# Layer 0's input projection of a streaming encoder as seven block products (Strassen's identity, one level)

## Chip, cores and metric

One Trainium2 chip, one core, one launch. The metric is the device time in microseconds of one execution. Engines: PE (TensorE) multiplies, DVE (VectorE), ACT (ScalarE) and POOL (GpSimd) work on elements, SP issues the transfers.

## What is computed

The reference is a two-layer encoder on 1088 tokens (1024 of a prompt, 64 of a running stream), D = 1024, everything in 32-bit floats. Layer 0 is a gated short convolution, layer 1 latent attention. The part that matters here is layer 0:

```
h = rms_norm(x, g)
b_gate, c_gate, xv, z = split(h @ w_in, 4)          # w_in: 1024 x 4096
u = c_gate * xv
conv = sum over k = 0..2 of u[t - 2 + k] * conv_w[k]
x1 = x + (silu(z) * b_gate * conv) @ w_out
```

The two rows of `u` before the first token are zeros for the prompt and a stored state for the stream.

## The kernel before

Tokens lie on the free axis, features on the 128 partitions (KD = 8 tiles of 128). A 32-bit factor is split into `hi` (cast to fp32r) and `lo` (the rest), and each product is three matmuls: hi by hi, hi by lo, lo by hi. `load_w` does this for weights: SP loads 512 KB into `wraw` (three buffers), ACT casts to `whi` (line 288), POOL subtracts into `wlo` (line 292).

Layer 0 takes the 1088 tokens in three chunks, `CHK`: 384, 384 and 320. For each of 8 feature tiles `ct` and each of 4 parts (order `PARTS = [1, 2, 3, 0]`: c_gate, xv, z, b_gate) `conv_mm` runs for each chunk 8 times 3 matmuls into one of 8 PSUM banks, taken in turn by `gps`; that is 2304 matmuls. `conv_evac` takes the bank to SBUF: lines 440 and 444 make `u`, 451 to 453 silu(z), 457 to 467 the convolution (462, 464) with its operands in SBUF, the gate (465) and the split into `YH`, `YL` (466, 467).

`XH`, `XL` hold x times the gain g; the factor 1 / rms per token, `rb`, multiplies the results afterwards. For the first `ct` the order is written out by hand (`keep_order`, `pe_order`): the chunks of x are loaded, split (391, 392), squared and summed (397 to 401), `rstd` finds the factor by Newton steps on three columns (320 to 330), and `spread` brings it back to the columns with products with the identity. Everywhere else in layer 0 a scheduler of the compiler orders the instructions within each engine.

Then `conv_out` (1024 x 1024, 8 tiles times 3 chunks), the residual, and layer 1 with its projections and attention (from line 576 on).

## Time and profile before

| | |
|---|---|
| time, median of 3 executions | 1116.86 us (1115.74 to 1117.88) |
| the profiled execution: span from first to last instruction | 1115.8 us |
| PE busy | 1075.0 us, 96% of the span |
| DVE, ACT, POOL busy | 56%, 45%, 37% |
| layer 0's input projection on PE | from 5.78 to 403.62 us |

For the profiled execution the profile has the span alone, no separate time; it lies within the three times above. PE's row counts from the start of a matmul to its modelled end, and matmuls overlap, so the distance between two starts is what a matmul costs in a stream. The granted clock stands beside the engines' times: 1.00 is 2.4 GHz, 0.50 is 1.2 GHz.

### The profile page before, as it was taken

To read this page: it belongs to the slowest core of one execution; us is meant where nothing else is said; L and a number is where in the kernel's file an instruction comes from. 1 tells how busy PE (TensorE), PEld (TensorE's weight loads), DVE (VectorE), ACT (ScalarE), POOL (GpSimd) and SP (SyncE) were. 2 spreads that over 40 slices of the span, in tenths; PEclk is the share of its full clock that TensorE was granted. 3 is DMA by queue.
4 is the path that set the end of the run, shared out by engine and by line. 5 is a ranking of instruction groups with operands and counts; after the bars stand their busy time and mean duration, and the time that the engine had idled before them with its cause. 6 is when DMAs were issued, how large, how long until landed. Compare 5 with 4: busy or idle time off the path is not lost.

```text
span 1115.8 us, 17727 instructions
## 1 busy us (share of the span) xinstructions
PE 1075.0 (96%) x6659; PEld 1033.5 (93%) x6659; DVE 626.8 (56%) x1277; ACT 502.7 (45%) x1077; POOL 407.5 (37%) x375
## 2 busy tenths in 40 slices
PE   8989999999999999999898999999999999999994
PEld 7989999999999999999798999899999999989983
DVE  6752222222322235554898442688888888896456
ACT  6512121221112133344442334777887778785452
POOL 3123232323324232122433232354555445463243
PEclk9989999999999999999998999999999999999997
DMA  6211111111112123322323113444323422434324
GB/s 228 67 38 39 57 38 43 53 38 50 46 38 77 40 78 139 137 94 90 105 101 124 48 35 86 119 91 103 68 59 91 95 61 51 104 123 151 99 83 153
DMA packets 45461, 93.18 MB, mean 84 GB/s; under 512 B 6672, under 2 KB 23824, under 8 KB 45376
## 3 DMA queue, kind: packets, MB, share of 16 engines
q1 hardware_dynamic: 45168, 91.73, 27.4%
q8 instruction: 52, 0.85, 0.3%
q14 instruction: 33, 0.27, 0.1%
q10 hardware_dynamic: 144, 0.26, 0.1%
q0 software_dynamic: 64, 0.07, 0.0%
...
## 4 chain that ended last, share of the span: by engine, by line
PE 75%; DVE 8%; issue 5%; ACT 4%; DMA 4%; POOL 2%; SPq 1%; POOLq 0%; DVEq 0%; ACTq 0%
PE PS L298 55%; PE PS L1088 16%; PE PS L1127 4%; DMA QB<-stg 2%; POOL wlo L1366 1%; DVE rb L401 1%; ACT PH L1140 1%; DVE PL L1144 1%; SPq L1214 1%; DVE OL L612 1%; DMA wraw<-in_w 1%; ACT stg L1204 1%; DVE qt L813 0%; DVE SZ L364 0%; DVE qt L818 0%
## 5 line engine op out<-in xcount | busy, mean ns | idle before, releaser
L298 PE MATMUL PS<-XH,whi 128*128 128x384 f32 (+1 forms) x984 | 324.2, 329 | 4.7 <-DVE SZ L632 3.9
L298 PE MATMUL PS<-XL,whi 128*128 128x384 f32 (+1 forms) x984 | 322.8, 328 | 0.8 <-DVE XL L392 0.8
L298 PE MATMUL PS<-XH,wlo 128*128 128x384 f32 (+1 forms) x984 | 321.3, 328 | 0.0
L292 POOL TENSOR_TENSOR wlo<-wraw,whi 128x1024 fp32r<-128x1024 f32 x56 | 135.9, 2427 | 301.0 <-ACT whi L288 297.9
L298 PEld LDWEIGHTS PS<-XH,whi 128*128 128x128 f32 x984 | 185.9, 189 | 6.1 <-issue 4.1
L298 PEld LDWEIGHTS PS<-XL,whi 128*128 128x128 f32 x984 | 185.9, 189 | 2.2 <-DVE XL L392 1.8
L298 PEld LDWEIGHTS PS<-XH,wlo 128*128 128x128 f32 x984 | 185.7, 189 | 0.2
L1088 PE MATMUL PS<-KB,QB 96*128 96x512 f32 (+11 forms) x576 | 125.1, 354 | 0.9 <-DVE SZ L632 0.6
L288 ACT CAST whi<-wraw 128x1024 fp32r<-128x1024 f32 (+1 forms) x57 | 59.3, 1040 | 140.4 <-PE PS L298 127.9
L1088 PEld LDWEIGHTS PS<-KB,QB 96*128 96x128 f32 (+1 forms) x576 | 94.4, 190 | 9.3 <-DVE PL L1144 1.1
L1105 DVE TENSOR_REDUCE st<-PS 128x1 f32<-128x1024 f32 (+7 forms) x128 | 94.6, 747 | 10.7 <-PE PS L1088 10.0
L1144 DVE TENSOR_TENSOR PL<-PS,PH 128x512 fp32r<-128x512 f32 (+3 forms) x192 | 98.8, 547 | 3.2 <-ACT PH L1140 1.8
L1122 POOL TENSOR_SCALAR Pt<-Pt,st 128x640 f32<-128x640 f32 (+3 forms) x64 | 61.4, 961 | 85.9 <-DVE st L1118 85.3
L1140 ACT CAST PH<-PS 128x512 fp32r<-128x512 f32 (+3 forms) x192 | 85.3, 496 | 14.6 <-PE PS L1127 13.2
L1088 PE MATMUL PS<-PH,VB 128*128 128x256 f32 x320 | 76.4, 278 | 0.1
L1088 PE MATMUL PS<-PL,VB 128*128 128x256 f32 x320 | 75.2, 281 | 0.2 <-DVE PL L1144 0.2
L1114 ACT ACTIVATE Pt<-PS,st 128x640 f32<-128x640 f32 (+3 forms) x64 | 62.0, 970 | 6.0 <-DVE st L1118 2.9
L298 PE MATMUL PS<-YL,whi 128*128 128x384 f32 (+1 forms) x192 | 63.0, 328 | 0.0
L298 PE MATMUL PS<-YH,whi 128*128 128x384 f32 (+1 forms) x192 | 63.0, 328 | 0.0
L298 PE MATMUL PS<-YH,wlo 128*128 128x384 f32 (+1 forms) x192 | 63.0, 328 | 0.0
L1088 PEld LDWEIGHTS PS<-PH,VB 128*128 128x128 f32 x320 | 60.7, 190 | 1.3 <-DVE PL L1144 0.8
L1088 PEld LDWEIGHTS PS<-PL,VB 128*128 128x128 f32 x320 | 61.0, 191 | 0.7 <-DVE PL L1144 0.4
...
## 6 DMA issues: line engine op xcount, KB each, us to landing
wraw<-in_w SPq DMA_DIRECT2D x64, 512.0 KB, 3.4
...
```

The costliest lines, as they stand in the source:

```text
L288: ins = A.copy(out=hi[:, :n], in_=raw[:, :n])
L292: ordered((lo_engine or G).tensor_sub(lo[:, :m], raw[:, :m], r32(hi[:, :m])))
L298: ins = PE.matmul(ps, lhsT, rhs, start=start, stop=stop)
L401: ordered(V.tensor_add(rb[:, c0:c1], rb[:, c0:c1], q))
L612: ordered((lo_engine or V).tensor_sub(lo, src, r32(hi)))
L1088: pin(PE.matmul(ps, lhsT, rhs, start=start, stop=stop))
L1105: pin(V.tensor_reduce(out=st[:, 0:1], in_=TL["S", h, i], axis=AX.XY, op=ALU.max, negate=True))
L1114: pin(A.activation(out=Pt, in_=TL.pop(("S", h, i)), func=AF.Exp, bias=st[:, 0:1], accum_out=st[:, 1:2]))
L1122: pin(G.tensor_scalar(Pt, Pt, st[:, 2:3], 1.0, op0=ALU.mult, op1=ALU.mult))
L1127: pin(PE.transpose(out=tp[:, j * P:(j + 1) * P], in_=TL["P", h, i][:, (j0 + j) * P:(j0 + j + 1) * P], identity=ident))
L1140: pin(A.copy(out=hi, in_=src))
L1144: pin(V.tensor_sub(lo, src, r32(hi)))
```

## The change

The product of a 1024-row weight and 1088 tokens is cut into blocks. The tokens become four quarters of `NS` = 272 columns; two quarters are a half, `sc` = 0 or 1. For one half and one pair of weight tiles (c_gate with xv, or z with b_gate) the 2 x 2 block product (8 blocks of 512 rows by 128 columns) is written with seven products, p1 to p7 (the form with 7 products whose sums share terms):

- `build` makes from the eight x tiles of a half the seven combinations of quarters and row halves, split in hi and lo (`SETS`); g and the factor rb are now multiplied into x first.
- `prep` makes for a pair the seven weight combinations: the casts of both raw tiles (`unit`), and three sums S1, S2, t4 with their own splits; S1 and S2 stand in PSUM banks 5 and 6.
- `product` runs 12 matmuls of 272 columns. p1, p6, p7 and p4 add up in one bank, and ACT copies the sum out after p1, p6 and p7; p5 and p3 share another bank. A block is finished with sums of a bank and a copy (`put`).
- `conv_tail` keeps the convolution's sum in PSUM bank 7.

`run` orders a pair's products p1, p5, (p3 of the pair before), p6, (p4 of the pair before), p2, p7, and puts behind each a step of the next pair's `prep` and a step of other work (`side`). The first half of tiles `ct` = 0 and 1 stays an ordinary product (in quarters); `build` of the first half runs beside `ct` = 1. Then come 28 pairs: 6 tiles times 2 for the first half, 8 times 2 for the second. The first half's result goes to DRAM and comes back (`reload_y`); the second half of x is loaded, squared and built during the first half's pairs (`second_half`). `rb` lies in `acc1`; x, the combinations and Y share two large regions. The residual's x is loaded and stored per chunk. 2736 matmuls of 272 columns replace 768 times (384 + 384 + 320).

```diff
-    def mm(ps, lhsT, rhs, start, stop):
-        ins = PE.matmul(ps, lhsT, rhs, start=start, stop=stop)
+    def mm(ps, lhsT, rhs, start, stop, more=False):
+        ins = PE.matmul(ps, lhsT, rhs, start=start, stop=stop, skip_group_check=more)
...
+    NS = T // 4
+    SC = 2 * NS
+    REG = 14 * 4 * NS
...
+    SETS = [[R[:, i * REG // 2:(i + 1) * REG // 2].rearrange("p (s k n) -> p s k n", s=7, k=4) for i in range(2)]
+            for R in (R2, R1)]
+    HS, LS = [R1[:, i * KD * SC:(i + 1) * KD * SC].rearrange("p (k n) -> p k n", n=SC) for i in range(2)]
+    rb = acc1
+    rb2 = [p1.tile([P, NS], F32, tag=x, name="rb2" + x, bufs=1) for x in ("kp1", "kp7")]
+    YLB = p1.tile([P, 2, T], F32R, name="YLB")
...
-            cv = p1.tile([P, 384], F32, tag="tC", name=nm("cv"), bufs=2)
-            ordered(V.tensor_mul(z[:, :n], ps_[:, :n], z[:, :n]))
+    def conv_tail(ct, sc, u, z, c):
+        a, b = c * NS, (c + 1) * NS
+        cv = PS[:, 7, :NS]
+        cw = [sm[:, C_CW + j * 8 + ct:C_CW + j * 8 + ct + 1] for j in range(3)]
+        ordered(A.activation(out=cv, in_=u[:, a:b], func=AF.Copy, scale=cw[0]))
+        for j in (1, 2):
+            ordered(V.scalar_tensor_tensor(cv, u[:, a + j:b + j], cw[j], cv, op0=ALU.mult, op1=ALU.add))
...
+        ordered(V.tensor_mul(y, cv, z[:, a:b]))
+        c0, c1 = sc * SC + a, sc * SC + b
+        if sc == 0:
+            SP.dma_start(out=y_d[ct][:, c0:c1], in_=y)
+        else:
+            A.copy(out=yh(ct, c0, c1), in_=y)
+            G.tensor_sub(yl(ct, c0, c1), y, r32(yh(ct, c0, c1)))
...
+    def reload_y():
+        for k in range(KD):
+            SP.dma_start(out=y, in_=y_d[k][:, :SC])
+            yield
+            A.copy(out=yh(k, 0, SC), in_=y)
+            G.tensor_sub(yl(k, 0, SC), y, r32(yh(k, 0, SC)))
+            yield
...
+    POS = dict(p1=0, p2=1, p4=2, p6=3, p7=4, p3=5, p5=6)
+    def build(sc, k):
+        h, l = [x[:, :, k] for x in SETS[sc]]
+        a, b = [STG[:, (2 * (k % 2) + i) * SC:(2 * (k % 2) + i + 1) * SC] for i in range(2)]
...
+        def put(s, x):
+            o, ol = h[:, s:s + 2], l[:, s:s + 2]
+            A.copy(out=o, in_=halves(x))
+            E.tensor_sub(ol, halves(x), r32(o))
+        if sc == 0:
+            build_dma(sc, k)
+        for x, kk in ((a, k), (b, k + 4)):
+            g = sm[:, C_NG + kk:C_NG + kk + 1]
+            if sc == 0:
+                V.scalar_tensor_tensor(x, x, g, rb[:, :SC], op0=ALU.mult, op1=ALU.mult)
+            else:
+                for c in range(2):
+                    t, y = PS[:, 7, :NS], x[:, c * NS:(c + 1) * NS]
+                    A.activation(out=t, in_=y, func=AF.Copy, scale=g)
+                    V.tensor_mul(y, t, rb[:, SC + c * NS:SC + (c + 1) * NS])
+                yield
+        yield
+        A.copy(out=h[:, 0], in_=a[:, :NS])
+        E.tensor_sub(l[:, 0], a[:, :NS], r32(h[:, 0]))
+        yield
+        put(1, b)
+        yield
+        E.tensor_add(b[:, NS:], a[:, NS:], b[:, NS:])
+        E.tensor_sub(a[:, NS:], a[:, :NS], a[:, NS:])
+        E.tensor_sub(a[:, :NS], b[:, NS:], a[:, :NS])
+        E.tensor_sub(b[:, :NS], b[:, :NS], a[:, :NS])
+        yield
+        put(3, a)
+        yield
+        put(5, b)
+        yield
+    jobs = []
...
+    def load_half():
+        slot = lambda k: STG[:, (k % 4) * SC:(k % 4 + 1) * SC]
+        for k in range(KD):
+            if k < 3:
+                SP.dma_start(out=slot(k), in_=xT[k][:, SC:])
+        yield
+        yield
+        for k in range(KD):
+            if k + 3 < KD:
+                SP.dma_start(out=slot(k + 3), in_=xT[k + 3][:, SC:])
+            if k == 0:
+                A.activation(out=rb[:, SC:], in_=slot(k), func=AF.Square)
+            else:
+                A.activation(out=slot(k), in_=slot(k), func=AF.Square)
+                G.tensor_add(rb[:, SC:], rb[:, SC:], slot(k))
+            yield
...
+    def parts_of(hi, lo, src, eng):
+        A.copy(out=hi, in_=src)
+        eng.tensor_sub(lo, src, r32(hi))
+        return hi, lo
+    def unit(src):
+        units[0] += 1
+        pool, tags, bufs = (p1, ("bhi", "blo"), 1) if units[0] % 3 == 0 else (wp[0], ("whi", "wlo"), 2)
+        return parts_of(*(pool.tile([P, 1024], F32R, tag=x, name=nm(x), bufs=bufs) for x in tags), src, G)
...
+    def prep(f):
+        ra, rb_ = raw(), raw()
+        SP.dma_start(out=ra, in_=f.srcs[0])
+        SP.dma_start(out=rb_, in_=f.srcs[1])
...
+        b12, b22 = rb_[:, :512], rb_[:, 512:]
+        b11, b21 = ra[:, :512], ra[:, 512:]
+        yield
+        give(unit(ra), "p1", "p2")
+        yield
+        A.copy(out=S1, in_=b12)
+        V.tensor_sub(b12, b22, S1)
+        V.tensor_sub(S1, S1, b11)
+        give(parts_of(*own(1), S1, V), "p5")
+        yield
+        V.tensor_sub(S2, b22, S1)
+        give(parts_of(*own(2), S2, V), "p6")
+        yield
+        t4 = p1.tile([P, 512], F32, tag="t4", name=nm("t4"), bufs=1)
+        V.tensor_sub(t4, b21, S2)
+        give(parts_of(*own(4), t4, G), "p4")
+        yield
+        give(unit(rb_), "p7", "p3")
+        yield
...
+    def product(f, name):
+        a, c = f.set, 3 + f.set
+        i = dict(p1=a, p6=a, p7=a, p4=a, p2=2, p5=c, p3=c)[name]
+        wh, wl = f.w[name]
+        ps = PS[:, i, :NS]
+        sh, sl = [x[:, POS[name]] for x in SETS[f.sc]]
+        new = name in ("p1", "p2", "p5")
+        for k in range(4):
+            ws = slice(k * P, (k + 1) * P)
+            mm(ps, wh[:, ws], sh[:, k], k == 0 and new, False, not new)
+            mm(ps, wh[:, ws], sl[:, k], False, False, not new)
+            mm(ps, wl[:, ws], sh[:, k], False, k == 3, not new)
+        if i == a and name != "p4":
+            t = p1.tile([P, NS], F32, tag="k" + name, name=nm(name), bufs=1)
+            A.copy(out=t, in_=ps)
+            if name == "p1":
+                f.p1 = t
+            if name == "p6":
+                f.p6 = t
+            if name == "p7":
+                f.put(22, 1, PS[:, c, :NS], t)
+        elif name == "p2":
+            f.put(11, 0, ps, f.p1)
+        elif name == "p4":
+            f.put(21, 1, ps, None)
+        elif name == "p3":
+            f.put(12, 0, ps, f.p6)
...
+                f.begin()
+            while f.whole and jobs:
+                side()
+            for name in ("p1", "p5", "p3", "p6", "p4", "p2", "p7"):
+                if name in ("p3", "p4"):
+                    if n:
+                        product(pairs[n - 1], name)
+                        if name == "p4":
+                            pairs[n - 1].end()
+                else:
+                    product(f, name)
+                step(n + 2 if name == "p7" else n + 1)
+                side()
+        product(pairs[-1], "p3")
+        product(pairs[-1], "p4")
+        pairs[-1].end()
+        while jobs:
+            side()
...
+        def put(o, silu, block, c, ps, x):
+            if block == 11 or block == 22:
+                V.tensor_add(o, ps, x)
+                if silu and block == 11:
+                    A.activation(out=o, in_=o, func=AF.Silu)
+                return
+            if x is not None:
+                V.tensor_add(ps, ps, x)
+            if silu and block == 21:
+                A.activation(out=ps, in_=ps, func=AF.Silu)
+            V.tensor_mul(o, ps, o)
...
-    for ct in range(KD):
-        u = p1.tile([P, SEQ + DEC + 4], F32, tag="u", name=nm("u"), bufs=2)
+        u, z = new_u(ct, 0), new_z()
+        if ct == 0:
...
-            for c in range(3):
+            for c in range(2):
...
+            jobs.extend(build(0, k) for k in range(4))
+        else:
+            for part in PARTS:
+                W = load_w(w1[ct][part], 1024)
+                for c in range(2):
+                    conv_evac(ct, u, z, part, c, conv_mm(c, W))
+                    side(2)
+    while jobs:
+        side()
...
+    def second_half():
+        yield from load_half()
+        yield from range(1, 5)
+        build_dma(1, 0)
+        build_dma(1, 1)
+        end = rstd([rb[:, SC:]], rb[:, SC:], D, SC)
+        yield from range(1, 12)
+        end()
+        yield from range(1, 3)
+        for k in range(4):
+            yield from build(1, k)
+            yield
+            if k < 2:
+                build_dma(1, k + 2)
+    jobs.append(second_half())
+    pairs = [f for sc, cts in ((0, range(2, KD)), (1, range(KD))) for ct in cts for f in conv_pairs(ct, sc)]
+    pairs[12].whole = True
+    run(pairs)
+    SP.dma_start(out=o_conv, in_=nconv.rearrange("p a b -> p (a b)"))
...
-        xr = p1.tile([P, T + 4], F32, tag="u", name=nm("xr"), bufs=2)
-        SP.dma_start(out=xr[:, :T], in_=xT[dt])
+        xr = new_x(dt)
+        for c, (c0, c1) in enumerate(CHK):
+            SP.dma_start(out=xr[c], in_=xT[dt][:, c0:c1])
```

The order of DVE where the first tile ends and the second begins: before (first fence), the end of the third chunk's evacuation (`rb_106` is the squared factor, `u`, `z`, `cv` the tiles of the text) and the second tile's first rows.

```order
L415 TENSOR_TENSOR rb_106<-rb 128x320
L440 TENSOR_TENSOR u_108<-PS,rb_106 128x256
L444 TENSOR_TENSOR u_108<-PS,u_108 128x256
L446 COPY nconv<-u_108 128x2
L451 TENSOR_TENSOR z_667<-PS,rb 128x320
L457 TENSOR_TENSOR z_667<-PS,z_667 128x320
L465 TENSOR_TENSOR cv_695<-cv_695,z_667 128x320
L472 MEMSET u_1070 128x2
```

and of the change, in the second tile (STG holds x of the half, R_104 the first half's combinations, acc_100 the factor):

```order
L518 TENSOR_TENSOR z_501<-PS,acc_100 128x272
L573 TENSOR_TENSOR STG<-STG 128x272
L559 SCALAR_TENSOR_TENSOR STG<-STG,sm,acc_100 128x544
L574 TENSOR_TENSOR STG<-STG 128x272
L575 TENSOR_TENSOR STG<-STG 128x272
L552 TENSOR_TENSOR R_104<-STG,R_104 128x2x272
L522 TENSOR_TENSOR z_501<-PS,z_501 128x272
L568 TENSOR_TENSOR R_104<-STG,R_104 128x272
L484 TENSOR_TENSOR y_740<-PS,z_501 128x272
```

Between the evacuations now stand `build`'s steps, whose tensors all lie in SBUF.

The order of ACT where the pairs begin, before (casts of weights and evacuations of the second tile):

```order
L288 CAST whi_876<-wraw_875 128x1024
L462 ACTIVATE cv_995<-u_706,sm 128x384
L462 ACTIVATE cv_1027<-u_706,sm 128x384
L288 CAST whi_966<-wraw_965 128x1024
L452 ACTIVATE z_905<-z_905 128x384
```

and of the change (604 and 606 are the squares of the second half's x, 551 casts of the first half's last combinations, 686 the copy after p1, 621 casts of weights):

```order
L621 CAST whi_833<-wraw_808 128x1024
L604 ACTIVATE acc_100<-STG 128x544
L686 COPY p_68_856<-PS 128x272
L606 ACTIVATE STG<-STG 128x544
L551 CAST R_104<-STG 128x2x272
L606 ACTIVATE STG<-STG 128x544
L551 CAST R_104<-STG 128x2x272
L621 CAST t2h_823<-PS 128x512
```

The last two casts of the first half's combinations now stand behind squares of tiles that are loaded into the slots that the combinations leave.

The order of POOL within the pairs: before, the rest of the second tile,

```order
L453 TENSOR_TENSOR z_961<-z_961,rb 128x320
L467 TENSOR_TENSOR YL<-cv_995,YH 128x384
L292 TENSOR_TENSOR wlo_1157<-wraw_1155,whi_1156 128x1024
L467 TENSOR_TENSOR YL<-cv_1059,YH 128x320
L292 TENSOR_TENSOR wlo_1241<-wraw_1239,whi_1240 128x1024
```

and of the change, while the second half is built (R_98 holds its combinations, the wlo, blo and t4l are weights):

```order
L622 TENSOR_TENSOR wlo_1348<-wraw_1254,whi_1347 128x1024
L568 TENSOR_TENSOR R_98<-STG,R_98 128x272
L552 TENSOR_TENSOR R_98<-STG,R_98 128x2x272
L572 TENSOR_TENSOR STG<-STG 128x272
L573 TENSOR_TENSOR STG<-STG 128x272
L574 TENSOR_TENSOR STG<-STG 128x272
L575 TENSOR_TENSOR STG<-STG 128x272
L622 TENSOR_TENSOR wlo_1413<-wraw_1387,whi_1412 128x1024
L552 TENSOR_TENSOR R_98<-STG,R_98 128x2x272 x2
L622 TENSOR_TENSOR t4l_1330<-t_131_1327,t4h_1329 128x512
```

Six steps of a `build` now stand between two weights' low parts.

## Rows read from the trace of the kernel before

**Rows 1.** The page: span, and busy time of each engine.

```profile
span 1115.8 us, 17727 instructions
PE 1075.0 (96%) x6659; PEld 1033.5 (93%) x6659; DVE 626.8 (56%) x1277; ACT 502.7 (45%) x1077; POOL 407.5 (37%) x375
```

**Rows 2.** Busy time by stretch: PE, PEld, DVE, ACT, POOL, PEclk, DMA share, GB/s.

```profile
5.78:80.00 74.22, 65.07 (x376) 62.29 (x375) 52.48 (x114) 34.87 (x69) 19.80 (x14) 0.95 0.34 112
80.00:403.62 323.62, 323.62 (x1970) 323.62 (x1969) 83.42 (x196) 62.18 (x96) 104.15 (x68) 1.00 0.15 48
...
700.00:1000.00 300.00, 295.98 (x2059) 273.93 (x2058) 252.17 (x581) 237.58 (x598) 155.62 (x208) 1.00 0.34 83
```

**Rows 3.** Timeline of PE: start us, duration us, engine, line, operation, tiles, shape.

```profile
5.78 0.42 PE L298 MATMUL PS<-XH,whi 128*128 128x384 f32 x1
...
352.66 0.31 PE L298 MATMUL PS<-XH,whi 128*128 128x320 f32 x1
...
356.18 0.34 PE L298 MATMUL PS<-XH,whi 128*128 128x384 f32 x1
...
364.52 0.31 PE L298 MATMUL PS<-XH,whi 128*128 128x320 f32 x1
...
403.62 0.33 PE L298 MATMUL PS<-YH,whi 128*128 128x384 f32 x1
```

**Rows 4.** Timeline of DVE and POOL in the first tile.

```profile
29.93 0.16 DVE L330 SCALAR_TENSOR_TENSOR rsy<-rst,rsy 128x3 f32<-128x3 f32 x1
...
33.02 0.61 DVE L392 SCALAR_TENSOR_TENSOR XL<-xst,sm,XH 128x384 fp32r<-128x384 f32 x1
33.55 0.55 DVE L401 TENSOR_TENSOR rb<-rb,sq 128x384 f32<-128x384 f32 x1
34.02 0.55 DVE L415 TENSOR_TENSOR rb<-rb 128x384 f32<-128x384 f32 x1
...
39.69 0.56 DVE L465 TENSOR_TENSOR cv<-cv,z 128x384 f32<-128x384 f32 x1
...
55.69 3.36 DVE L464 SCALAR_TENSOR_TENSOR cv<-u,sm,cv 128x384 f32<-128x384 f32 x2
...
61.31 2.26 DVE L330 SCALAR_TENSOR_TENSOR rsy<-rst,rsy 128x3 f32<-128x3 f32 x1
...
55.61 2.38 POOL L292 TENSOR_TENSOR wlo<-wraw,whi 128x1024 fp32r<-128x1024 f32 x1 [0.42 <-ACT whi L288]
...
61.22 2.34 POOL L292 TENSOR_TENSOR wlo<-wraw,whi 128x1024 fp32r<-128x1024 f32 x1
```

**Rows 5.** Timeline of PE around its longest wait there.

```profile
64.81 1.65 PE L298 MATMUL PS<-ident,rsy 128*128 128x128 f32 x6 [4.38 <-DVE rsy L330]
66.11 0.61 PE L298 MATMUL PS<-XH,YH 128*128 128x320 f32 x1
...
70.22 0.31 PE L298 MATMUL PS<-XH,YH 128*128 128x320 f32 x1
```

**Rows 6.** Groups by line and shape: busy us, mean ns | idle before, releaser.

```profile
L444 DVE TENSOR_TENSOR u<-PS,u 128x384 f32<-128x384 f32 x14 | 7.8, 558 | 36.5 <-PE PS L298 36.5
L1144 DVE TENSOR_TENSOR PL<-PS,PH 128x512 fp32r<-128x512 f32 x96 | 64.1, 682 | 2.9 <-ACT PH L1140 1.8
...
L288 ACT CAST whi<-wraw 128x1024 fp32r<-128x1024 f32 x56 | 58.8, 1049 | 139.2 <-PE PS L298 127.9 <-issue 11.1 <-DMA wraw<-in_w 0.2
L1140 ACT CAST PH<-PS 128x512 fp32r<-128x512 f32 x96 | 55.7, 603 | 10.3 <-PE PS L1127 9.3
L466 ACT CAST YH<-cv 128x320 fp32r<-128x320 f32 x6 | 2.8, 460 | 0.9 <-DVE cv L465 0.2
...
L292 POOL TENSOR_TENSOR wlo<-wraw,whi 128x1024 fp32r<-128x1024 f32 x27 | 64.8, 2398 | 150.0 <-ACT whi L288 150.0
L467 POOL TENSOR_TENSOR YL<-cv,YH 128x384 fp32r<-128x384 f32 x13 | 13.2, 1018 | 34.7 <-ACT YH L466 34.7
```

**Rows 7.** DMA issues: KB each, us from issue to landing.

```profile
wraw<-in_w SPq DMA_DIRECT2D x64, 512.0 KB, 3.4
```

More of the change, by code (lines that the diff above doesn't have):

```diff
@@ new lines, in new_u, with new_z, build_dma @@
+    def new_u(ct, sc):
+        u = p1.tile([P, SC + 4], F32, tag="u", name=nm("u"), bufs=1)
+        if sc == 0:
+            V.memset(u[:, 0:2], 0.0)
+        return u
+    def new_z():
+        return p1.tile([P, SC], F32, tag="z", name=nm("z"), bufs=1)
+    POS = dict(p1=0, p2=1, p4=2, p6=3, p7=4, p3=5, p5=6)
+    def build_dma(sc, k):
+        for i in range(2):
+            o = (2 * (k % 2) + i) * SC
+            SP.dma_start(out=STG[:, o:o + SC], in_=xT[k + 4 * i][:, sc * SC:(sc + 1) * SC])
@@ new lines, with side @@
+    jobs = []
+    def side(n=1):
+        while n and jobs:
+            if next(jobs[0], 0) == 0:
+                jobs.pop(0)
+            else:
+                n -= 1
+    def load_half():
[14 more added lines that the diff above has]
+            yield
@@ new lines, with raw, own, give @@
+    raws = [0]
+    def raw():
+        raws[0] += 1
+        pool, tag, bufs = (p1, "braw", 1) if raws[0] % 4 == 0 else (wp[0], "wraw", 3)
+        return pool.tile([P, 1024], F32, tag=tag, name=nm(tag), bufs=bufs)
+    def prep(f):
+        ra, rb_ = raw(), raw()
+        SP.dma_start(out=ra, in_=f.srcs[0])
+        SP.dma_start(out=rb_, in_=f.srcs[1])
+        w = f.w = {}
+        S1, S2 = PS[:, 5, :512], PS[:, 6, :512]
+        def own(i):
+            return [p1.tile([P, 512], F32R, tag=f"t{i}{x}", name=nm(f"t{i}{x}"), bufs=1) for x in "hl"]
+        def give(u, *names):
+            for j, n in enumerate(names):
+                w[n] = [x[:, j * 512:(j + 1) * 512] for x in u]
+        b12, b22 = rb_[:, :512], rb_[:, 512:]
[17 more added lines that the diff above has]
+        yield
@@ new lines, in run, with step @@
+    def run(pairs):
+        steps = {}
+        for n, f in enumerate(pairs):
+            f.set = n % 2
+        def step(n, k=1):
+            for _ in range(k):
+                if n < len(pairs):
+                    if n not in steps:
+                        steps[n] = prep(pairs[n])
+                    next(steps[n], None)
+        step(0, 6)
+        step(1, 1)
+        for n, f in enumerate(pairs):
+            if f.begin:
+                f.begin()
[7 more added lines that the diff above has]
+                            pairs[n - 1].end()
+                else:
+                    product(f, name)
[6 more added lines that the diff above has]
+            side()
@@ L475 @@
+    PARTS = [1, 2, 3, 0]
+    for ct in range(2):
+        u, z = new_u(ct, 0), new_z()
         if ct == 0:
@@ L497 @@
             pe_order[0] = True
-            held = {c: [] for c in range(3)}
+            held = {c: [] for c in range(2)}
             held[0].append(conv_mm(0, W[1], 3))
```

210 lines of the change are left out of this document (127 added, 83 removed).

## The prediction

> **What bounds the kernel now.** I read the page first: PE is busy 96% of 1115.8 us [rows 1], so the time is what PE's stream costs plus the places where it stands still. Then the table by stretch [rows 2]: from 80 us to the end of the input projection at 403.62 us PE is busy 323.62 of 323.62 us at a granted clock of 1.00, while DVE has 26%, ACT 19% and POOL 32% to do. In this stage every matmul column taken away is time, and the element engines have room. From 5.78 to 80 us it is otherwise: PE is busy 65.07 of 74.22 us at clock 0.95, and DVE is at 71%.
>
> What a matmul costs I take from starts on PE's timeline [rows 3]: 24 matmuls of 320 columns from 352.66 to 356.18, 146.7 ns each, and 48 of 384 columns from 356.18 to 364.52, 173.8 ns each. Together that is one feature tile and part, 11.86 us; 32 of them are 379.5 us. The stage lasts 403.62 - 5.78 = 397.8 us, so 18.3 us of it are start.
>
> **PE's work after the change.** No row has 272 columns. The line through the two widths gives 126.4 ns, and a constant cost per column (384 to 272 in proportion) would give 123.1 ns; I take 126.5, since the two measured widths show a fixed part. 2736 x 126.5 ns = 346.1 us, against 379.5: **33.4 us less**. A product of 12 matmuls is 1.52 us, a pair of seven 10.63 us. The order counts 2736 matmuls, so that the change leaves the products in place is ruled out. The Trainium skill, in "TensorE: Matmul & The Clock Gate", section "Back-to-back issue gap", gives columns / 2.4 + 2.5 ns for the isolated gap at the fast clock; by it the three widths would cost 162.5, 135.8 and 115.8 ns, and the work would fall by 37.1 us. The rows show some 13 ns of fixed part where the page has 2.5, so here the finer cut pays less.
>
> **The start, which the change makes longer.** First tile: the narrower quarters shorten DVE's rows. In a stream on DVE a scalar_tensor_tensor of 384 columns starts 0.53 us before its successor, a tensor_tensor 0.47 us (starts at 33.02, 33.55 and 34.02) [rows 4]; at 0.97 ns a column, the slope between the 384 and 512 groups (558 and 682 ns) [rows 6], that is 0.42 and 0.36 us for 272, 0.69 and 0.63 for 544, 0.60 for 512. DVE ended the first factor at 29.93 + 0.16 and the first chunk's gate (465) at 40.25 us [rows 4]; with 272 columns I get about 29.2 and 38.5 us. New is who waits: the convolution's sum stands in bank 7, and so does, in turn, the second quarter's xv product. It must wait until DVE has read the sum, so PE, done with the product before it at about 33 us, stands for some 5 us. Before, the longest stand was 4.38 us, for DVE's Newton steps [rows 5], and behind it 320-column matmuls came 270 ns apart until 70.2 (clock 0.5, [rows 5]): 1.9 us lost. I charge about the same again. The second factor then reaches DVE at about 48.5 us, and PE ends the second tile at about 75 us.
>
> Then the first half's combinations. p5, the second product, needs all four `build`s. Its chain is DVE's. From 48.5 us DVE has four builds (each 2 x 0.69 + 3 x 0.63 + 5 x 0.36 = 5.07 us, 20.3 in all), 22 evacuations of 272 columns (18 of 0.36 and 4 of 0.42, 8.1 us) and four weight differences (2.4 us): 30.8 us. Beside it POOL makes five low parts of weights, 2.40 us each [rows 6]. What such a subtraction does to DVE shows in [rows 4]: the pair of 464 rows took 3.36 us beside one that started 0.08 us before them, in place of about 1.2, and a three-column step took 2.26 us in place of 0.16. Both DVE rows read two operands from SBUF. Line 444, with one operand in PSUM, has a mean of 558 ns [rows 6], which is 384 columns at DVE's rate and a fixed part, so it shows no such wait. Builds read SBUF only. A third of DVE's time there is rows with PSUM, which pass: 12.0 x 2/3 = 8 us. Bounds: 0 if every subtraction meets PSUM rows, 12 if none does. Last the hand-offs: `build` 2 and 3 load into slots that earlier ones leave, 3.4 us per load [rows 7], and the last two casts on ACT stand behind squares of tiles loaded after that, one of them behind two loads in turn. I take 6 us (0 to 10). So p5 starts at 48.5 + 30.8 + 8 + 6 = 93.3 us, 18 us after the second tile; p1 fills 1.5 of them. The clock is then down; I charge 2 us as in [rows 5].
>
> **The pairs.** From p5 on 195 products remain: 195 x 1.518 = 296.0 us if PE never waits. Per pair DVE has six rows of 512 and five of 272, with the convolution every second time: 6.6 us of 10.63. ACT has two casts of 1024 (1049 ns), four of 512 (603 ns), three copies of about 0.42 us (460 ns at 320 columns less 48 columns) and half of silu and convolution, 7.4 us. POOL has 2 x 2.40 + 1.3 = 6.1 us, and about 0.8 us of y's low part per pair in the second half [rows 6]. The weight preparation and the copies are so covered, with two products (3.0 us) between a sum and its copy's reader. Without that cover each pair would cost PE ACT's and DVE's chain, some 2 us. What is least covered: while the second half is built, POOL has another 8 us per build, which takes nine slots (13.7 us), so it is nearly full; the low part of the next pair's first weights is due first. In the attention PE loses 1.3% (295.98 of 300 us) with DVE at 84% and ACT at 79% [rows 2]; I take that as a model, 4 us, and 1 us for POOL: **5 us**, bounds 0 and 20. At the end p3 waits for p7's copy and sum, 1.3 us, since no next pair stands between. SP's queue gains y's stores, their reload and the x loads; with four raw buffers a load of 3.4 us [rows 7] has a pair's time, so I charge nothing; without it the pair's first cast would be late by what a load exceeds 10 us. The convolution's state copies are ACT rows of two columns. The residual's loads per chunk, and its program order on PE, run under 24 matmuls each: nothing.
>
> **The sum.** The projection ends at 93.3 + 296.0 + 2 + 1.3 + 5 = 397.6 us, against 403.62: 6 us earlier. Of 33.4 us, 23 are given back at the start, and 4 to 5 in the pairs. Layer 1 has the same products in the same order. The profiled execution would span 1109.8 us; its span lies 1.1 us under the median of the executions, so I forecast **1111 us** (about 1104 to 1117 for this case).
>
> **Rivals.**
>
> *The builds hide better.* If DVE's waits for POOL fall into waits that it has anyway (4 us left in place of 8), the hand-offs cost 3, and the pairs lose 3, p5 starts at 86.3 us and the end comes 9 us earlier: 1102 us. For it: DVE is at 71% in the old start, with free stretches. Against: after 48.5 us it has a queue, not gaps. Chance 0.22.
>
> *The pairs wait.* ACT's queue is in order: a cast of t1 or t2 waits for DVE, which waits for ACT's copy of S1; and p1's, p6's and p7's copies queue behind such casts. Place: PE at the first matmul of p6 and p7. Price: whatever a copy is later than 3.0 us, 28 times. It decides from 6 / 28 = 0.21 us more per pair than I charge; at 0.6 us per pair it is 16.8 us, and the time 1128 us. For it: a pair has five hops between ACT and DVE; against it: 60 to 70% load, and the attention, which hops as often. The Trainium skill, in the same page's section "A second HAM failure mode: psum-queue depth-cycling", says that short stands between groups that turn through PSUM banks can make the clock swing between its two levels. No run here shows that: from 80 to 403.62 us eight banks turn at clock 1.00. If it held for a tenth of the pairs' 296 us, another 15 us would go, the same place. Chance 0.24.
>
> *The changeover takes longer.* If builds, POOL and the late squares line up badly (12 and 10 us in place of 8 and 6) and the first pairs lose another 4 us behind loads, the end is 12 us later than forecast: 1123 us. Chance 0.16.
>
> **How the numbers follow.** My forecast keeps 0.38. A measurement of this kernel can tell about 0.2%, 2.2 us, from no change. Faster by more: most of the forecast's case (0.33) and the first rival (0.22), 0.55. Slower: most of the second (0.20) and third (0.12), 0.32. Within: what is left, 0.13. The range goes from a little under the first rival to the second, 1099 to 1128; what lies outside is a start that hides wholly and pairs that wait over 0.6 us. The forecast's own range is 1104 to 1117.
>
> **What would show it.** In the changed profile: matmuls of 272 columns 126 to 127 ns apart; p5's first matmul near 93 us, with a stand of over 10 us in front of it whose releaser is DVE's low part (line 552) or ACT's cast (551); DVE's build rows over 2 us long beside POOL's; a stand of some 5 us near 35 us that DVE's line 484 ends; pairs 10.6 to 10.9 us apart. A pair of over 11.2 us, or the clock below 1.00 past 110 us, shows the second rival; p5 before 87 us the first.

## The result, and the profile after

The changed kernel takes 1141.82 us (1139.30 to 1142.36) against 1116.75 (four executions of each): a ratio of 1.0223, interval 1.0208 to 1.0237. It is 25 us slower; I forecast 6 us faster, and a range to 1128. The page of the changed kernel:

```profile
span 1140.6 us, 19740 instructions
PE 1060.4 (93%) x7099; PEld 1010.8 (89%) x7099; DVE 769.5 (67%) x1530; ACT 645.8 (57%) x1402; POOL 541.7 (47%) x454
```

PE is busy 15 us less than in [rows 1], in a span that is 25 us longer: the work went down, the stands went up. PE's timeline tells where:

```profile
38.91 0.82 PE L299 MATMUL PS<-R,whi 128*128 128x272 f32 x2 [6.09 <-DVE y L484]
...
96.00 0.66 PE L299 MATMUL PS<-R,t2h 128*128 128x272 f32 x2
...
415.95 0.41 PE L299 MATMUL PS<-R,bhi 128*128 128x272 f32 x2
...
417.45 0.29 PE L299 MATMUL PS<-R,t2h 128*128 128x272 f32 x1
...
427.78 0.51 PE L299 MATMUL PS<-R,whi 128*128 128x384 f32 x2
```

From 415.95 to 417.45 lies one product, 1.50 us or 125 ns a matmul (forecast 126.5). The third product, p6 of the first pair, starts at 96.00 (94.8 by the forecast). The projection ends at 427.78, where I had 397.6; before it was 403.62 [rows 3]. Behind it nothing changed: 712.8 us to the end of the span, 712.2 before. So of the 30.2 us between forecast and run, 1.2 arose before p6 and 29.0 behind it, in the pairs. Counted by starts: from p6 to the end 2328 matmuls of 125 ns are 291.0 us; the forecast had 302.8 us there, the run 331.8. So 40.8 us are lost where 11.8 were charged. By stretch (columns as in [rows 2]; the last two rows are two of four short stretches at the slow clock):

```profile
96.00:216.00 120.00, 106.38 (x774) 104.00 (x774) 73.69 (x158) 72.31 (x141) 90.95 (x64) 0.94 0.41 129
216.00:427.78 211.78, 201.56 (x1578) 198.47 (x1576) 132.05 (x273) 125.32 (x266) 134.26 (x79) 1.00 0.33 102
...
96.00:101.00 5.00, 5.00 (x24) 5.00 (x24) 2.32 (x4) 2.72 (x6) 2.25 (x2) 0.50 0.69 232
128.33:131.74 3.41, 3.41 (x17) 3.41 (x16) 0.20 (x1) 0.52 (x2) 0.00 (x0) 0.50 0.86 282
```

PE stands 13.6 us in the first 120 us of pairs and 10.2 in the other 212: 23.8 where I charged 5. In the first part the second half is loaded and built. The page counts a stand from the modelled end of a matmul; by starts the stands took some 28 of the 40.8 us. In the first part the clock also falls three times to 0.50 for 3.4 us; a matmul then takes 0.23 us instead of 0.125, so that one such stretch costs some 1.5 us, and the three cost 4.6. The rest are the end of the drop at the start, short gaps, and 20 small matmuls of the second half's factor. Who ended PE's waits from 96 to 428 us (what waited, for whom: us in all, times, longest):

```profile
PE PS L299 <- DVE z L753: 10.1, 10, 1.9
PE PS L299 <- ACT p L686: 4.9, 4, 2.4
PE PS L299 <- DVE z L745: 4.4, 3, 2.7
PE PS L299 <- DVE u L745: 3.4, 3, 2.1
PE PS L299 <- ACT acc L344: 0.7, 1, 0.7
```

Three quarters are sums of `put` on DVE (745, 753) that give PE a bank back. They need 0.44 us each. Why they come late shows the timeline ahead of one stand of 2.68 us:

```profile
189.60 2.39 POOL L622 TENSOR_TENSOR wlo<-wraw,whi 128x1024 fp32r<-128x1024 f32 x1
...
191.94 0.77 POOL L575 TENSOR_TENSOR STG<-STG 128x272 f32<-128x272 f32 x1
192.67 1.37 POOL L552 TENSOR_TENSOR R<-STG,R 128x544 fp32r<-128x544 f32 x1
...
193.99 1.30 POOL L622 TENSOR_TENSOR t4l<-t,t4h 128x512 fp32r<-128x512 f32 x1
...
195.33 0.69 DVE L666 TENSOR_TENSOR t<-wraw,PS 128x512 f32<-128x512 f32 x1 [5.24 <-POOL t4l L622]
195.93 0.43 DVE L745 TENSOR_TENSOR z<-PS,p 128x272 f32<-128x272 f32 x1
...
196.40 0.43 ACT L747 ACTIVATE z<-z 128x272 f32<-128x272 f32 x1 [1.56 <-DVE z L745]
...
197.18 0.38 ACT L686 COPY p<-PS 128x272 f32<-128x272 f32 x1
...
197.63 0.43 DVE L745 TENSOR_TENSOR z<-PS,p 128x272 f32<-128x272 f32 x1
...
198.12 0.52 PE L299 MATMUL PS<-R,whi 128*128 128x272 f32 x2 [2.68 <-DVE z L745]
```

DVE's row of t4 (666) writes the one tile t4, so it waits until POOL has made the low part of the pair before (t4l). POOL is at a weight and at the second half's builds. DVE works in order: the first sum 745 stands behind 666, which waited 5.2 us. ACT works in order too: its silu (747) waits for that sum, and the copy after p7 (686) comes behind it. The second sum 745 needs that copy, and it is the one that gives PE its bank. All 28 rows of 666 (the mean, the idle time ahead of them and what ended it):

```profile
L666 DVE TENSOR_TENSOR t<-wraw,PS 128x512 f32<-128x512 f32 x28 | 19.2, 687 | 31.5 <-POOL t4l L622 31.5
```

### The profile page after: what moved, and what is told of

Its sections match the earlier page's. It is cut to its first block, busy times and chain, and to the rows that moved or that the text cites. A ratio compares the mean times of both kernels' runs of the same rounds, so it can differ in the third digit from the quotient of the medians.

```text
span 1140.6 us, 19740 instructions
## 1 busy us (share of the span) xinstructions
PE 1060.4 (93%) x7099; PEld 1010.8 (89%) x7099; DVE 769.5 (67%) x1530; ACT 645.8 (57%) x1402; POOL 541.7 (47%) x454
## 4 chain that ended last, share of the span: by engine, by line
PE 58%; DVE 8%; issue 6%; POOL 5%; DMA 4%; ACT 4%; SPq 1%; POOLq 0%; ACTq 0%; DVEq 0%
PE PS L299 39%; PE PS L1430 15%; PE PS L1469 4%; DMA QB<-stg 3%; POOL wlo L1708 1%; POOL t4l L622 1%; POOL wlo L622 1%; ACT PH L1482 1%; ACT stg L1546 1%; DVE OL L954 1%; DVE t L666 1%; SPq L1556 1%; DVE PL L1486 0%; DVE qt L1155 0%; DVE SZ L365 0%
## 5 line engine op out<-in xcount | busy, mean ns | idle before, releaser
L299 PE MATMUL PS<-R,whi 128*128 128x272 f32 (+2 forms) x1598 | 368.7, 315 | 30.5 <-DVE z L753 7.7
L299 PEld LDWEIGHTS PS<-R,whi 128*128 128x128 f32 x1598 | 272.0, 192 | 37.6 <-DVE z L753 9.0
L299 PE MATMUL PS<-R,wlo 128*128 128x272 f32 (+2 forms) x856 | 267.5, 314 | 4.8 <-POOL wlo L622 3.6
L299 PEld LDWEIGHTS PS<-R,wlo 128*128 128x128 f32 x856 | 163.6, 192 | 5.7 <-POOL wlo L622 3.8
L292 POOL TENSOR_TENSOR wlo<-wraw,whi 128x1024 fp32r<-128x1024 f32 x32 | 78.8, 2463 | 184.7 <-ACT whi L288 178.8
L1447 DVE TENSOR_REDUCE st<-PS 128x1 f32<-128x1024 f32 (+7 forms) x128 | 94.7, 749 | 11.2 <-PE PS L1430 10.4
L622 POOL TENSOR_TENSOR wlo<-wraw,whi 128x1024 fp32r<-128x1024 f32 x28 | 67.6, 2414 | 49.5 <-ACT whi L621 49.5
L299 PE MATMUL PS<-R,bhi 128*128 128x272 f32 x320 | 62.1, 292 | 5.0 <-DVE z L753 2.4
L288 ACT CAST whi<-wraw 128x1024 fp32r<-128x1024 f32 (+1 forms) x33 | 34.1, 1032 | 46.2 <-PE PS L299 23.2
L299 PEld LDWEIGHTS PS<-R,bhi 128*128 128x128 f32 x320 | 50.3, 191 | 6.3 <-DVE z L753 3.3
L1469 PE MATMUL PS<-ident,Pt 128*128 128x128 f32 x416 | 55.4, 273 | 0.2 <-ACT Pt L1456 0.2
L1464 POOL TENSOR_SCALAR Ph<-Ph,st 128x512 f32<-128x512 f32 (+3 forms) x64 | 34.2, 535 | 39.0 <-DVE st L1460 28.6
```

Of the source, the lines that this page charges most:

```text
L288: ins = A.copy(out=hi[:, :n], in_=raw[:, :n])
L292: ordered((lo_engine or G).tensor_sub(lo[:, :m], raw[:, :m], r32(hi[:, :m])))
L299: ins = PE.matmul(ps, lhsT, rhs, start=start, stop=stop, skip_group_check=more)
L622: eng.tensor_sub(lo, src, r32(hi))
L1447: pin(V.tensor_reduce(out=st[:, 0:1], in_=TL["S", h, i], axis=AX.XY, op=ALU.max, negate=True))
L1464: pin(G.tensor_scalar(Pt, Pt, st[:, 2:3], 1.0, op0=ALU.mult, op1=ALU.mult))
```

## Experiments

Every time is a median beside runs of the kernel before on the same chip (1116.7 to 1117.2 us); the ratio is to these. Where two experiments ran on different chips, their difference carries the 0.5 us between these medians.

**1. t4's step later.** In `prep`:

```diff
-        t4 = p1.tile([P, 512], F32, tag="t4", name=nm("t4"), bufs=1)
-        V.tensor_sub(t4, b21, S2)
-        give(parts_of(*own(4), t4, G), "p4")
-        yield
         give(unit(rb_), "p7", "p3")
         yield
+        yield
+        t4 = p1.tile([P, 512], F32, tag="t4", name=nm("t4"), bufs=1)
+        V.tensor_sub(t4, b21, S2)
+        give(parts_of(*own(4), t4, G), "p4")
+        yield
...
-        step(0, 6)
+        step(0, 7)
```

> The step of t4 (DVE's difference, ACT's cast, POOL's low part) moves from behind p6 to behind p2; nothing else changes. Theory A, DVE's queue: the sums that free PE's banks (745, 753) stand behind t4's row, which waits for POOL's low part of the pair before. Then most of the 18 us of stands that 745 and 753 end go, and with them the three drops of the clock (5 us): the projection ends at 405 to 412 us instead of 427.8, the time is 1119 to 1127. Theory B, too much work beside the pairs: the stands keep their sum (20 us or more) and another row ends them, the time is 1138 to 1142. Theory C, two products of cover are too short for copy and sum: as B in the steady pairs, 0.6 to 1.6 us in each second pair after 220 us.

One more thing changes with it: the cast and the low part of the pair's second raw tile (`unit(rb_)`) come one place earlier, behind p6 instead of p4.

1134.98 us, 1.0162 (1.0145 to 1.0179): 6.8 us faster, less than theory A had. In the steady pairs the stands fall from 10.2 to 6.4 us (215.64 to 420.97 us). DVE's wait for t4l went from 31.5 to 17.7 us only:

```profile
L669 DVE TENSOR_TENSOR t<-wraw,PS 128x512 f32<-128x512 f32 x28 | 19.2, 686 | 18.2 <-POOL t4l L622 17.7
```

**2. No second half.** `second_half` zeroes the rest of its region and does nothing else.

> The second half's x is not loaded, squared, scaled, combined or split; its products read what stands in the region (with the rest zeroed by POOL), so the second half's result is left out. Theory B: the 12.6 us of stands from 96 to 213 us and the drops of the clock go, 16 to 20 us: the time is 1121 to 1126, and the steady pairs keep their 11 us. Theory A: POOL's queue is what makes t4 late, so the first ten pairs come down to the steady pairs' loss (about 0.5 us a pair, 5 us), 12 to 15 us: 1126 to 1130. If the builds cost nothing, 1139 to 1142.

1122.91 us, 1.0060 (1.0043 to 1.0077): 18.9 us faster. In 120 us PE now stands 4.3 us, and POOL falls from 91 to 65 us:

```profile
94.40:214.40 120.00, 115.73 (x899) 114.42 (x899) 75.84 (x155) 66.14 (x124) 64.55 (x32) 0.99 0.37 116
```

This takes away the second half's load, squares and scaling together with its builds. All of that, which I had covered with 1 us for POOL, is the largest part ("the builds" below); the steady pairs keep 8.6 us.

**3. Ordinary products in banks 0 to 6.**

```diff
+    split_psum(g=(0, 7))
     for ct in range(2):
```

> The ordinary products of the first two tiles take turns in banks 0 to 6, so none has the bank of the convolution's sum. The prediction's step on the start: the stand of 6.1 us at 33 to 39 us goes and the clock stays at 1.00 there (2 us); the sum of squares behind it on PE, and so the second factor and the builds, come that much earlier: p5 runs at about 88 us instead of 95, the time is 1133 to 1136. Rival: the loads of x and DVE hold the second factor anyway, or POOL's low parts hold the builds: 0 to 2 us, 1139 to 1142.

1131.55 us, 1.0131 (1.0116 to 1.0146): 10.3 us faster, somewhat more than the forecast's step. p5 and p6 start at

```profile
85.88 0.82 PE L299 MATMUL PS<-R,t1h 128*128 128x272 f32 x2 [6.25 <-ACT t1h L621]
89.04 0.65 PE L299 MATMUL PS<-R,t2h 128*128 128x272 f32 x2
```

instead of 96.00 for p6: the wait for the convolution's bank delayed the sum of squares behind it on PE (DVE's first row of the second factor, 321, starts at 39.44 us instead of 44.60), and with that all builds.

**4. The convolution's sum in SBUF** (on top of experiment 3).

```diff
-        cv = PS[:, 7, :NS]
+        y = p1.tile([P, NS], F32, tag="cv", name=nm("y"), bufs=1)
+        cv = y
...
-        y = p1.tile([P, NS], F32, tag="cv", name=nm("y"), bufs=1)
```

> As the kernel with banks 0 to 6, and the convolution's sum stands in SBUF (in y's own tile) instead of bank 7, as it did before the change: it undoes one of the two passes through PSUM. If rows of DVE with two operands in SBUF wait for POOL's subtractions as in the profile before (up to 2.4 us for one row), the rows of 474 and 484 get longer, each pair of z loses 1 to 2 us, and the time is 14 to 28 us over the kernel with banks 0 to 6 alone. If DVE has the room, within 3 us of it.

1162.93 us, 1.0415 (1.0400 to 1.0431): 31.4 us slower than experiment 3. The same rows of DVE in the pairs, with the sum in PSUM (experiment 3):

```profile
L474 DVE SCALAR_TENSOR_TENSOR PS<-u,sm,PS 128x272 f32<-128x272 f32 x56 | 28.0, 500 | 3.9 <-ACT PS L472 3.6
L484 DVE TENSOR_TENSOR y<-PS,z 128x272 f32<-128x272 f32 x28 | 12.3, 440 | 1.0
```

and in SBUF:

```profile
L475 DVE SCALAR_TENSOR_TENSOR y<-u,sm,y 128x272 f32<-128x272 f32 x54 | 68.2, 1264 | 3.4 <-ACT y L473 2.6
L484 DVE TENSOR_TENSOR y<-y,z 128x272 f32<-128x272 f32 x27 | 32.6, 1206 | 0.7
```

The rows are 2.5 and 2.7 times as long: with both operands in SBUF they wait for POOL (where POOL is idle such a row takes 0.43 us; the rows are shown with the account of the start below). That pass through PSUM is worth 31 us to the changed kernel.

**5. Experiments 1 and 3 together.**

> Both edits together: t4's step behind p2, and ordinary products in banks 0 to 6. They touch different stretches (pairs, start), so by theory A and the prediction's start the gains add: 1141.8 - 6.8 - 10.3 = 1124.7, range 1122 to 1127. If the later start of the pairs had only hidden t4's late part, less: 1128 to 1132.

1125.20 us, 1.0077 (1.0060 to 1.0093): the gains add. This kernel is the base of the next four.

**6. Three ordinary tiles** (`range(3)`, pairs from tile 3 on).

> As the kernel with both edits, and a third tile of the first half stays an ordinary product, so that the first half's combinations have 24 us more behind ordinary products. It costs 24 more matmuls, 3.0 us, and the second half's builds have 70 places in the pairs instead of 84. If p5's wait for DVE's build chain (the 11 us of stands before p5 and the clock's drop behind them) is what the start loses, 5 to 9 us faster than both edits alone; if the builds are slowed by POOL's low parts just as long, or the second half's builds lose as much in fewer places, 0 to 4 us slower.

1126.31 us, 1.0091 (1.0074 to 1.0108), no gain. p6 starts at 108.1 us; 87.7 and one tile of 192 matmuls (24.1 us) would be 111.8, so the start got 3.7 us back, for 3.0 us of matmuls, and the pairs lost 1 us more.

**7. Builds of the second half in 14 places** (five more `yield`s in `build` and behind it).

> As the kernel with both edits, and each build of the second half takes 14 places between products instead of 9 (the same rows, more room). Theory B': POOL has more work than time there, 8 us of build and 7.9 of weights in 13.7 us; with 21 us it fits: the stands of the first ten pairs and their drops of the clock fall by half or more, 5 to 9 us faster than both edits alone. Rival: what costs is each meeting of a build's row with a weight's row, however spread: 0 to 2 us.

1126.70 us, 1.0085 (1.0062 to 1.0107): no gain. Room alone does not help.

**8. DVE makes all of the second half's builds** (`E = V`).

> As the kernel with both edits, and DVE instead of POOL makes the second half's differences, sums and low parts (3 rows of 544 and 5 of 272 for each of four builds). Theory B': POOL's queue falls under its time, ACT's casts and t4's low part come sooner, but DVE's rows read SBUF alone and wait for POOL's subtractions as in the first half's build (10 us in 4 builds); PE feels a part of that: 3 to 8 us faster than both edits alone. Rival, all three engines are simply too busy there: no gain, or 2 to 6 us slower, as DVE serves PE's banks.

1124.71 us, 1.0074 (1.0059 to 1.0089): no gain; in the first 120 us of pairs PE now waits 9.8 us for u's sums on DVE (746) and no longer for ACT's copies.

**9. Two tiles for t4** (on top of 5).

```diff
-        t4 = p1.tile([P, 512], F32, tag="t4", name=nm("t4"), bufs=1)
+        t4 = acc1[:, :512] if f.set else p1.tile([P, 512], F32, tag="t4", name=nm("t4"), bufs=1)
```

> As the kernel with both edits, and t4 takes turns in two tiles (the second is the first half's factor, which is done with by then), so that DVE's row of t4 waits for POOL's low part of two pairs ago instead of the last one. With both edits alone DVE still stands there for up to 5.2 us while the second half is built, and 746's sums behind it. Theory A: these stands (5 to 8 us of the 12.4 in the first 120 us of pairs) go, and the one drop of the clock there: 1117 to 1121. Theory B' (POOL's queue itself makes PE wait, by ACT's casts behind it): 1123 to 1126, the stands are then ended by ACT's copies (687).

1119.59 us, 1.0024 (1.0012 to 1.0036): 5.6 us faster than 5. DVE's wait for t4l is gone:

```profile
L669 DVE TENSOR_TENSOR acc<-wraw,PS 128x512 f32<-128x512 f32 x14 | 9.5, 679 | 0.0
L669 DVE TENSOR_TENSOR t<-wraw,PS 128x512 f32<-128x512 f32 x14 | 9.5, 678 | 0.0
```

The steady pairs now stand 1.7 us in all, so theory A holds for them. In the first 120 us PE still stands 12.8 us, but ACT's copies end over half of that, as theory B' had it (the waits of all pairs; those for 687 all lie in the first 120 us):

```profile
PE PS L299 <- ACT p L687: 6.9, 5, 3.2
PE PS L299 <- DVE z L746: 4.6, 3, 2.7
```

**10 and 11. Two tiles and 14 places; two tiles and another order of the first pair.**

> As the kernel with two tiles of t4, and the builds of the second half take 14 places instead of 9. If DVE's wait for t4 was what ate the room in the stretched kernel, the room now shows: 2 to 5 us faster than two tiles of t4 alone, ACT's casts (551) wait less for POOL's rows. If POOL's rows cost the same however spread: within 1.5 us of it.

> As the kernel with two tiles of t4, and the first pair alone runs p1, p2, p6, p5, p7 instead of p1, p5, p6, p2, p7: the combination of p5 is the last that each build makes, those of p2 and p6 come earlier. If p5's wait (6.3 us with banks 0 to 6) is for the builds' end, p2 and p6 fill up to 3.0 us of it: 2 to 4 us faster than two tiles of t4 alone. If it is for the weight difference t1 (ACT's cast, DVE's low part) and t2 comes later still: 0 to 1 us.

1122.55 us, 1.0059 (1.0041 to 1.0077), and 1120.62 us, 1.0029 (1.0018 to 1.0040). Neither helps. More places cost 3 us. In the profile of 10 the clock falls to 0.50 three times in the pairs, each time for 3.4 us (at 159.7, 183.6 and 210.9 us), in that of 9 once, which is some 3 us; why it falls more often stays open. Experiment 7 has the same three drops against one in 5. With the other order p6 waits 6.7 us for the cast of t2 where p5 had waited 6.3 for that of t1.

**12. DVE makes the four sums of a second-half build** (`V` for `E` in 572 to 575, on top of 9).

> As the kernel with two tiles of t4, and DVE instead of POOL makes the four sums and differences of quarters (572 to 575) in the second half's builds; the low parts stay on POOL. In the kernel with two tiles of t4, ACT's cast of a combination (551) stands up to 4.0 us for these rows of POOL, and ACT's copies that PE needs (687) and the cast of t2 stand behind it. If that queue is what the builds cost, 4 to 9 us faster than two tiles of t4 alone, 1111 to 1116, and 687 ends under 2 us of stands between 88 and 208 us. If DVE's rows, which read SBUF alone, wait for POOL's subtractions in turn (up to 2.4 us each, and PE's sums behind them), 0 to 4 us slower.

1116.17 us, 0.9997 (0.9988 to 1.0006): 3.4 us faster than 9. Both sides were right in part. ACT's copies end only 1.0 us of the stands between 88 and 208 us, but DVE's rows now wait for POOL:

```profile
153.20 2.39 POOL L622 TENSOR_TENSOR wlo<-wraw,whi 128x1024 fp32r<-128x1024 f32 x1
153.28 2.60 DVE L572 TENSOR_TENSOR STG<-STG 128x272 f32<-128x272 f32 x1 [1.47 <-POOL R L552]
...
157.16 0.43 DVE L746 TENSOR_TENSOR z<-PS,p 128x272 f32<-128x272 f32 x1
...
157.65 0.52 PE L299 MATMUL PS<-R,bhi 128*128 128x272 f32 x2 [2.80 <-DVE z L746]
```

**13. Two tiles and no second half.**

> As the kernel with two tiles of t4, and without the second half's load, squares, scaling and builds (its result is left out, as in the first such kernel). It shows what the builds still cost once DVE no longer waits for t4's low part. If the 18.9 us that they cost in the changed kernel were mostly DVE's wait for t4, the two kernels lie 5 to 8 us apart: 1112 to 1115. If ACT's and POOL's queues hold most of it, 12 to 17 us apart: 1103 to 1108.

1100.35 us, 0.9851 (0.9834 to 0.9867): 19.2 us under experiment 9, more than either forecast allowed, and as much as the builds cost in the changed kernel. So DVE's wait for t4 was a loss beside theirs, not the way in which they cost. In the pairs PE then never stands for 120 us:

```profile
87.70:207.70 120.00, 120.00 (x957) 120.00 (x957) 79.75 (x165) 72.14 (x133) 68.75 (x35) 1.00 0.36 121
```

**14. The same four sums with one operand in PSUM, in three places** (on top of 9, in the second half's builds alone, `sc` = 1).

```diff
-        E.tensor_add(b[:, NS:], a[:, NS:], b[:, NS:])
-        E.tensor_sub(a[:, NS:], a[:, :NS], a[:, NS:])
-        E.tensor_sub(a[:, :NS], b[:, NS:], a[:, :NS])
-        E.tensor_sub(b[:, :NS], b[:, :NS], a[:, :NS])
+        if sc:
+            t = PS[:, 7, :NS]
+            A.copy(out=t, in_=b[:, NS:])
+            V.tensor_add(b[:, NS:], t, a[:, NS:])
+            yield
+            A.copy(out=t, in_=a[:, :NS])
+            V.tensor_sub(a[:, NS:], t, a[:, NS:])
+            V.tensor_sub(a[:, :NS], b[:, NS:], t)
+            yield
+            A.copy(out=t, in_=b[:, :NS])
+            V.tensor_sub(b[:, :NS], t, a[:, :NS])
+        else:
+            E.tensor_add(b[:, NS:], a[:, NS:], b[:, NS:])
+            E.tensor_sub(a[:, NS:], a[:, :NS], a[:, NS:])
+            E.tensor_sub(a[:, :NS], b[:, NS:], a[:, :NS])
+            E.tensor_sub(b[:, :NS], b[:, :NS], a[:, :NS])
```

> As the kernel with DVE's rows in the second half's builds, but each of the four sums takes one operand from PSUM: ACT copies three quarters into bank 7 first, in three places between products instead of one. In the kernel with DVE's rows such a row took up to 2.6 us beside POOL's subtraction, with PE standing 2.8 and 3.9 us behind. If that wait is bound to two operands in SBUF, the rows take 0.43 us, these stands go and the time is 1109 to 1113. If the three extra hops between ACT and DVE cost as much, 1115 to 1118.

1103.81 us, 0.9883 (0.9870 to 0.9897): 12.4 us faster than 12, and 13 us faster than the kernel before. PE stands 3.0 us in the first 120 us of pairs, and the clock stays up but for the last of its drop at the start:

```profile
87.00:207.00 120.00, 117.00 (x920) 115.83 (x920) 90.76 (x200) 85.35 (x173) 90.11 (x54) 0.99 0.45 146
207.00:389.80 182.80, 181.08 (x1432) 179.84 (x1431) 116.68 (x246) 114.42 (x243) 122.16 (x73) 1.00 0.33 107
```

DVE is busier than in the changed kernel (91 us against 74 in the first 120 us of pairs) and PE waits less. **16** keeps the three places and takes the operand back to SBUF.

> The fastest kernel so far (1103.8 us) with its second-half rows on DVE in the same three places, but again with both operands in SBUF and no copies by ACT: it parts the operand's place from the spacing. If PSUM is what counts, such rows take up to 2.6 us beside POOL again and the time is 1112 to 1117; if the three places are what counts, 1102 to 1106, as ACT has three copies less.

1114.25 us, 0.9981 (0.9969 to 0.9993): 10.4 of the 12.4 us are the operand's place, and some 2 the three places. The first and last sum of a build in 16 (the slow ones):

```profile
L578 DVE TENSOR_TENSOR STG<-STG 128x272 f32<-128x272 f32 x4 | 6.8, 1693 | 0.0
L573 DVE TENSOR_TENSOR STG<-STG 128x272 f32<-128x272 f32 x4 | 6.0, 1512 | 5.6 <-POOL R L552 5.6
```

and in 14:

```profile
L575 DVE TENSOR_TENSOR STG<-PS,STG 128x272 f32<-128x272 f32 x4 | 1.8, 442 | 6.4 <-POOL R L552 6.4
L582 DVE TENSOR_TENSOR STG<-PS,STG 128x272 f32<-128x272 f32 x4 | 1.7, 436 | 0.5 <-ACT PS L581 0.5
```

**15. The same in both halves' builds, in one place.**

> The same for the builds of both halves, all in one place of a build. In the first half's builds DVE's rows of 572 to 575 are half of those that waited for POOL's low parts (some 5 us in all before p5). If p5 waits for DVE, it comes 3 to 5 us earlier and the time is 2 to 4 us under the kernel with the second half's rows alone; if the convolution's sum, which has bank 7 too, holds the rows, or the hops do, it is 0 to 4 us over it.

1118.50 us, 1.0017 (1.0008 to 1.0026), 15 us slower than 14. The rows are as short (0.44 us), but all copies and sums of a build stand in one place, and PE stands 10.2 us in the first 120 us of pairs. At the start p5 begins at 78.7 us instead of 83.8, but its later parts wait for the builds, and p6 is no earlier (87.95 instead of 86.96). The two changes in it were not tried apart.

**17. The edit of 14 alone, on the changed kernel.**

> The changed kernel with this one edit alone (the second half's sums on DVE, one operand from PSUM, in three places; t4's step, its one tile and bank 7 as in the change). The builds cost 18.9 us there, and the edit took 15.8 us of 19.2 in the kernel with the other three. If the two losses are separate, 1124 to 1128; if DVE's wait for t4's low part also grows with POOL's queue, which this edit shortens, some of that goes too: 1119 to 1124.

1127.91 us, 1.0103 (1.0083 to 1.0123): 13.9 us faster than the changed kernel; on top of 9 it took 15.8. So the builds' loss and DVE's wait for t4 are nearly separate; of that wait 24.2 us are left, of 31.5.

## Why the prediction was wrong

- **PE's work: right.** 2736 matmuls at 125 instead of 126.5 ns: 3 to 4 us better than charged.
- **The start: right within 1.2 us, in part by errors that cancel.** The stand for bank 7 was 6.09 us (5 forecast), and the clock's drop lasted from p6 until 101 us, 5.0 us at 0.50, of which some 2.2 are lost (2 forecast). The second factor reached DVE at 50.5 us (48.5 forecast), POOL's subtractions made DVE's rows some 10.8 us longer (8 forecast), and DVE stood idle only 2.8 us where I had 6 for hand-offs. p5 itself started at 88.10 us (93.3 forecast) and then waited for its weight's low part and the last combinations, so the stand of over 10 us that I named as a sign came in four pieces (3.6, 1.4, 1.6 and 3.6 us). DVE's rows waited for POOL's subtractions as forecast (the first row below has no row of POOL beside it):

```profile
55.80 0.43 DVE L572 TENSOR_TENSOR STG<-STG 128x272 f32<-128x272 f32 x1
...
77.28 2.39 POOL L622 TENSOR_TENSOR blo<-wraw,bhi 128x1024 fp32r<-128x1024 f32 x1 [1.50 <-ACT bhi L621]
77.30 2.95 DVE L559 SCALAR_TENSOR_TENSOR STG<-STG,sm,acc 128x544 f32<-128x544 f32 x1
79.61 2.84 POOL L622 TENSOR_TENSOR wlo<-wraw,whi 128x1024 fp32r<-128x1024 f32 x1
80.18 2.57 DVE L574 TENSOR_TENSOR STG<-STG 128x272 f32<-128x272 f32 x1
```

  By the Trainium skill, "SBUF — State Buffer", section "Who interferes with whom", an instruction of DVE with two inputs from SBUF contends with a GpSimd one that reads SBUF, and one with at most one such input, outside DVE's two-port modes, does not. The runs agree: 1264 against 500 ns in experiments 4 and 3, 1512 against 442 in 16 and 14.
- **The pairs: the step that failed**, "I take that as a model, 4 us, and 1 us for POOL: 5 us". The runs showed 23.8 us of stands and 4.6 us in three drops of the clock. I compared each engine's load with a pair's time, and took from 60 to 70% of load that the rows would be in time. No sum of loads shows a row that waits: 666 is 0.69 us of DVE's time, and held DVE 31.5 us, as its one tile was still read by POOL. That was to be seen in the order, where t4 has one buffer and its reader is POOL. Experiments 1 and 9 take it away, 12.4 us together (experiment 1 also moves a weight's low part, which was not tried apart).
- **POOL in the builds**: my own figures were 8 us of build and, at 6.1 us a pair, 7.9 us of weights in nine places of 1.52 us: 15.9 in 13.7 us, more than full, where I wrote nearly full and charged 1 us. The builds cost 18.9 us (experiment 2). Yet POOL was not full: from 140 to 220 us it was busy 65.9 of 80 us, as a build began only every 16 to 20 us. And more places did not help (7, 10). What counted was who stands behind POOL's rows, ACT's casts and, through them, the copies that PE needs. With the sums on DVE, one operand in PSUM and three places, 15.8 of 19.2 us come back (14).
- **The rivals.** "The pairs wait" (0.24) came nearest in time and was half right in place. It had p1's, p6's and p7's copies late behind casts of t1 or t2. The copies themselves end 4.9 of 23.5 us; in the stand shown above p7's copy was late too, but behind a silu that waited for DVE and t4. With all these copies and hops in place, but without the second half's builds, PE does not stand in 120 us of pairs (13), so a cover of two products was enough there. The range ended at this rival's 0.6 us a pair. The stands of the page alone were 23.8 us in 28 pairs, 0.85 us each, and without the three drops of the clock the time would still be about 1137 us (an estimate, 1141.8 - 4.6). Beside this rival stood a rule of the clock, short stands between groups that turn through PSUM banks. It is from the Trainium skill, "TensorE: Matmul & The Clock Gate", section "A second HAM failure mode: psum-queue depth-cycling". The trace agrees in part: in the first 120 us there are three drops, right behind stands of 1.8 to 2.1 us, but two longer stands, of 2.4 and 2.7 us, had none right behind them. They cost 4.6 us in place of the 15 that I worked out; behind 216 us, with stands up to 1.6 us, the clock stayed at 1.00.
- **The rest: right.** The tail waited 1.01 us (1.3), and nothing moved behind the projection.

Against experiment 14, the changed kernel has three parts to its loss: bank 7 in the first tiles (10.3 us alone), t4's place and tile (12.4) and the builds' sums on POOL (15.8). Together they are 38.5 us; the two kernels lie 38.0 us apart. Most of these were measured one on top of the other, so the agreement adds little: it says that the first two gains, measured alone, add. Where some of PE's work is saved, these are what has to be out of its way.
